# The last norm of a mixture-of-experts block beside the last four experts instead of the last two

## The chip, the cores and the metric

The kernel runs on one core of one Trainium2 chip. The metric is the device time of one execution in microseconds (us), here the median of several runs. The core has five engines with queues of their own: TensorE (PE, matrix products), VectorE (DVE), ScalarE (ACT), GpSimd (POOL) and SyncE (SP, which here only issues DMAs). The profile calls the loading of a product's fixed operand PEld.

## The reference

One block with 2048 tokens of 1024 columns: a mixer (Hyena filters and Fourier mixing), then a hierarchical mixture of experts, then a last norm. Only the last two parts matter here:

```python
g_sel = jnp.argmax(g_logits, axis=-1)                       # one group of 4 for each token
e_logits = jnp.take_along_axis(e_logits, g_sel[:, None, None], axis=1)[:, 0]
top_l, top_i = lax.top_k(e_logits, TOP_K)                   # two of this group's 8 experts
weight = p_group[:, None] * jax.nn.softmax(top_l, axis=-1)
...
    a = xb @ w_gate[e]
    u = xb @ w_up[e]
    y = (jax.nn.silu(a) * u) @ w_down[e]
    return (y * rows_w[:, None].astype(y.dtype)).astype(tok.dtype)
...
x = x + hierarchical_moe(rmsnorm(x, norm2_g[i]), ...)
return rmsnorm(x, final_g)
```

Both choices of a token lie in one group. So two experts of different groups never have a token in common. There are 32 experts with 6 MB of weights each (float32).

## The kernel before

The mixer and the routing take the first half of the span. The routing counts each expert's tokens and sorts the experts by their counts (`order`, on the DVE): the first turns are fixed (experts 0 and 1), the following have many and few tokens in a mixed order, and the last `NLAST` = 2 turns go to the experts with the fewest. An expert has 128 slots for tokens; the ranks below 18 have 32 slots more (`over` and the products L1583 and L1637).

The experts run turn after turn. Turn e, part 0 (`gate_up`) is 8 chunks of weights, part 1 (`down`) is 4; a chunk is 128 x 1024 numbers, 512 KB. The list `turns` sets the order: part 0 of an expert comes before part 1 of the one before it, so that the transposes of an expert's result (`turn_s`) fall into the other's products. At the end before, this order is given up: (29,1), (30,0), (30,1), (31,0), (31,1), with `turn_s` right behind `gate_up`.

`take` hands out the next chunk. At each call it runs one step of the list `ends` if there is one, issues loads for up to 28 chunks ahead on SP's queue, and cuts the chunk that is two ahead. A cut (L1391, L1392) splits float32 into two parts for exact products: ACT writes the high part h, then the low part l = w - h is written by the DVE, or by POOL for the chunks of `POOL_CUTS` and `TAIL_CUTS` (every second chunk from 360 on). Each chunk then takes six products of 128 x 128 by 128 x 512. A loaded chunk lies in one of 24 buffers: of every 24 chunks the first 16 in the ring with the tag `wr`, 8 in two other rings. The buffer is free when the chunk is cut.

An expert's result is added to the rows of X2 (in DRAM) with an indirect DMA by POOL (L1650; L1652 for the tokens beyond 128). These scatter-adds wait for each other.

The last norm is made for all tokens in `bulk`, called when the last expert but two has added its rows: for each of 16 tiles a read of X2 into a `wr` buffer (L1437, on SP), a sum of squares (L1427, on ACT), for each four tiles a short chain of small operations (`rsq`, L242 to L256), a product with the scale and the gain on the DVE (L1453) and a write to the output (L1454, on SP). These are steps in `ends`, so they run beside the last experts' products. The last two experts' tokens get their sums and norm again: `ahead` gathers the rows of X2 (L1472), `finish` adds the product (L1482), writes the sums to X2 (L1483) and norms (L1484, L1486), and at the very end the rows are scattered to the output (L1705). The second of them may share tokens with the first, so its `ahead` comes after the first one's sums.

After all experts a loop runs over blocks of tokens beyond all slots; it has as many rounds as there are such blocks.

The order on each engine and the buffers of a ring are fixed when the program is built, by priority in program order among what is ready; the waits between engines are put in then.

Of the kernel before, what the change touches and what calls it, by code (L numbers as in the profile page):

```python
# [45 lines left out]
# experts are taken by their counts: the first ones get 32 slots beyond the 128  # L46
NFIX = 2
# the first experts' 128 slots take tokens of the first tiles only
FIRST = 14
NLAST = 2  # L50
# [4 lines left out]
TAIL_CUTS = tuple(range(360, 384, 2))  # L55
# [6 lines left out]
def _ranks():  # L62
    """The rank by count of the expert at each turn."""
    n, few = NE - NFIX - NLAST, NE - NOV - NLAST
    many, rest = iter(range(NFIX, NOV)), iter(range(NOV, NE))
    mid = [next(rest) if (i + 1) * few // n > i * few // n else next(many) for i in range(n)]
    return list(range(NFIX)) + mid + list(rest)
# [18 lines left out]
def fft_tables(T):  # L86
    """A transform of 4096 points in two stages: n = 64 a + p, p = 16 m + g, k = r + 64 k2.

    The first one sums over a and turns by exp(-2 pi i r n / 4096), r = 0..31 (r = 0 stands for 0 and 32, both
    real before the turn); the second one sums over p.  # L90
    """
# [11 lines left out]
    w = first(64 * a[None, :, None] + 16 * m[None, None, :] + g[:, None, None])     # [g, a, m, comp]  # L103
    wu = np.zeros((16, 2, 2, 32, 2, 2, 2, 64))      # [g, m % 2, part of z, a, m // 2, pass, m % 2, comp]
# [9 lines left out]
    w = first(32 * np.arange(P)[None, :] + np.arange(32)[:, None]).reshape(32, 64, 2, 64)     # [q, a, x, comp]  # L114
# [25 lines left out]
    # the inverse leaves p in the order 4 g + m  # L140
# [5 lines left out]
def tables():  # L146
# [16 lines left out]
    # real and imaginary parts of a 64-point transform, two groups at once  # L163
# [6 lines left out]
    # transform over t, folded twice: t < 512, bins k = 2 k' + parity  # L170
# [14 lines left out]
    # routing: tokens, counted from one, in the order of their tiles; rows of ranks  # L185
# [6 lines left out]
    # order of the experts: their numbers as tie breakers, ranks of the turns, masks  # L192
# [14 lines left out]
def build(tc, I, out, dbg=None, upto=99):  # L207
# [4 lines left out]
    with es:  # L212
# [8 lines left out]
        # Fourier columns of tiles 0..3 and 8..11; those of tiles 15 - k and 7 - k, with the row that follows, are read backwards  # L221
# [16 lines left out]
        def rsq(dst, src, scale, pool, n, tag, ln=False):  # L238
            """dst = (src * scale + EPS) ** -0.5"""
# [9 lines left out]
            # one Newton step for what the tables leave  # L249
# [8 lines left out]
        # ------------------------------------------------------------------ mixer, first part  # L258
# [15 lines left out]
        with ExitStack() as e1, ExitStack() as e2:  # L274
# [52 lines left out]
            def conv(c, wvec, sink):  # L327
                """Projection chunk c through the short filter, a quarter of t for every call; sink(q, piece)."""
# [33 lines left out]
            def to_rows(src, dst):  # L362
                """[channel, 512 t] to [t, channel] rows of DRAM, in one or two parts, after the next products."""
# [16 lines left out]
            def sinks(c):  # L380
                """Filter and use of chunk c: v (8..11) is kept for x1 (4..7), whose product with it is z."""
# [13 lines left out]
            with tc.tile_pool(name="pa", bufs=1) as pa:  # L395
                # per-channel vectors: short filter (3 x 12), its bias (12), gains of heads and of the first norm
# [57 lines left out]
            def wprime(g):  # L454
                """Fourier columns of the projection, with the transform along a head folded in."""
# [28 lines left out]
            def ktaps(q):  # L484
                """The filter's taps 32 i + q, and the absolute sum so far."""
# [30 lines left out]
            def ksum(kt):  # L516
                """The kernel's absolute sum; the skip weight goes in as a tap at lag 0."""
# [32 lines left out]
            # implicit filters' features: partitions = (half of t, feature)  # L550
# [46 lines left out]
            def spread():  # L597
                """Features of t on the lower half of the partitions, of 2048 - t on the upper one."""
# [44 lines left out]
            def fweights(h):  # L643
                """Weights of half h of the Fourier columns, in two parts."""
# [8 lines left out]
            def fourier(h, i, wh, wl, pm, dst=None):  # L653
                """Fourier columns of tile i, rows = t, to DRAM or to where they are used."""
# [68 lines left out]
            def prod(o, w, xh, xl):  # L723
                """o = w x, both in two parts."""
# [3 lines left out]
            def residue(n):  # L728
# [6 lines left out]
                if n == 0:  # L735
                    # the real bins 0 and 32 and those between them
# [8 lines left out]
                else:  # L745
                    # real parts on the lower half of the partitions, imaginary ones on the upper half
# [35 lines left out]
            def begin(t):  # L782
                """Rows t and 1024 + t of the fold, the first half of the columns where the second one comes straight."""
# [9 lines left out]
            def pair(t):  # L793
                """Sums and differences of rows t and L - t, and of 1024 + t and 1024 - t."""
                rr = rrs.pop(t)
                pq = []
                for k in range(2):
                    # groups of 66 real parts and 62 imaginary ones
# [9 lines left out]
            # Fourier columns, rows = t  # L808
# [41 lines left out]
        # ------------------------------------------------------------------ Fourier mixing, output projection  # L850
        seq = []
        z = NE - NLAST
        turns = [(0, 0)] + [t for e in range(1, z) for t in ((e, 0), (e - 1, 1))]
        turns += [(z - 1, 1), (z, 0), (z, 1), (z + 1, 0), (z + 1, 1)]
# [33 lines left out]
        def gather(e, part=(0, 1)):  # L888
# [4 lines left out]
            if 1 in part and RANK[e] < NOV:  # L893
# [3 lines left out]
                if e < NFIX:  # L897
                    # the queue goes on with these cuts while the rows are unknown
# [3 lines left out]
        # the first gathers come before the last tiles' rows  # L902
# [5 lines left out]
        with ExitStack() as e3:  # L908
# [21 lines left out]
            def headnorm(pool, y, n=P, ln=False):  # L930
                """y [n, 8, 64] in place: every head over its root mean square."""
# [10 lines left out]
            def split_T(pool, y, rev=False):  # L942
                """[t, 512] to hi and lo of its transpose, [128 c, 4, 128 t]."""
# [11 lines left out]
            def mix(yh, yl, wh, wl, h):  # L955
                """Half h of the output columns."""
# [33 lines left out]
            with tc.tile_pool(name="fo", bufs=1, side="right", reuse_waits="tile") as fo:  # L990
# [9 lines left out]
                # t = 512, which is its own partner  # L1000
# [14 lines left out]
                def fold(t, par):  # L1015
                    """Parity par of the bins wants the sum and the difference, the other one the difference and the sum."""
# [94 lines left out]
            with tc.tile_pool(name="pd", bufs=1, side="right", reuse_waits="tile") as pd_:  # L1111
# [11 lines left out]
                # a token's number in two parts and its weight in three, which bfloat16 holds exactly  # L1123
# [27 lines left out]
                def first_rows(dst, src, u):  # L1151
                    """Rows to gather: a slot's token, or the quarter of it that a partition holds."""
# [5 lines left out]
                def order():  # L1158
                    """Experts by their counts: one-hot of the turn of each, and what depends on it."""
# [7 lines left out]
                    V.scalar_tensor_tensor(so[:, 0], cnt, float(NE), srt[:, 0:NE], op0=ALU.mult, op1=ALU.add)  # L1167
                    V.tensor_tensor(so[:, 1], so[:, 0], srt[:, 2 * NE:3 * NE], op=ALU.mult)
# [14 lines left out]
                def route(o0, n):  # L1183
                    """Experts, ranks and slots of n tiles from o0 on."""
# [3 lines left out]
                    def first(src, w, rev, tag):  # L1188
                        """One-hot of the first largest of w."""
# [24 lines left out]
                    # weights of the two choices  # L1214
# [33 lines left out]
                    # an expert's slots get their tokens and weights: one-hot of the rank against that of the expert  # L1248
# [20 lines left out]
                    if o0 + n == FIRST:  # L1269
                        # later tokens of the first experts get no rank below 128  # L1270
# [24 lines left out]
                        # rows to add to; an empty slot adds nothing to a row of its own  # L1295
# [6 lines left out]
                    for k in range(2):  # L1302
                        # the choice's number among all ranks
# [78 lines left out]
        # ------------------------------------------------------------------ experts  # L1382
        if True:
# [3 lines left out]
            def cut(n):  # L1387
# [4 lines left out]
                x = (G if n in POOL_CUTS + TAIL_CUTS else V).tensor_tensor(l, raws[n], h, op=ALU.subtract)  # L1392
# [6 lines left out]
            def take():  # L1399
                """The next chunk of weights; those after it are loaded and cut ahead."""  # L1400
# [28 lines left out]
            def bulk():  # L1429
                """The last norm of all tokens, in steps; those of the experts still at work get theirs again."""  # L1430
# [8 lines left out]
                def sq(o):  # L1439
# [4 lines left out]
                    # the weights' cuts go first  # L1444
# [5 lines left out]
                def scale(o):  # L1450
                    g, n = of[o]
                    x = xts.pop(o)
                    V.scalar_tensor_tensor(x, x, fss[g][1][:, o - g:o - g + 1], fgb, op0=ALU.mult, op1=ALU.mult)  # L1453
                    S.dma_start(out[0, P * o:P * o + P, :], x)  # L1454

                def step(k):
                    for o in range(2 * k, min(2 * k + 2, NT)):
                        read(o)
                    if 0 <= k - 6 < NT:
                        sq(k - 6)  # L1460
                    for o in range(2):
                        if scales:
                            scale(scales.pop(0))
                return [lambda k=k: step(k) for k in range(30)]
# [3 lines left out]

            def ahead(e):
# [352 lines left out]
```

## Time and profile before

| | us |
|---|---|
| median of 3 runs | 1753.75 (1752.33 to 1755.37) |
| profiled execution, first to last instruction (span) | 1749.5 |
| median of the runs above the span | 4.25 |
| PE busy | 1622.4 (93%) |
| DVE busy | 1228.6 (70%) |
| ACT busy | 1040.4 (59%) |
| POOL busy | 477.4 (27%) |

The page gives no time for the profiled execution but its span; what lies around it is taken as 4.25 us, the difference to the median. A group in the profile names its line, engine and operation, then what is written and read, how many there are, their busy time, the mean of one in ns, and the idle time of the engine just before them with what ended it. A row of the timeline begins with its start from the beginning of the span, then its length. Where an engine is held by another, the wait is inside the length that the row shows, not in front of it.

### The profile page before, as it was taken

To read this page: it belongs to the slowest core of one execution; us is meant where nothing else is said; L and a number is where in the kernel's file an instruction comes from. 1 tells how busy PE (TensorE), PEld (TensorE's weight loads), DVE (VectorE), ACT (ScalarE), POOL (GpSimd) and SP (SyncE) were. 2 spreads that over 40 slices of the span, in tenths; PEclk is the share of its full clock that TensorE was granted. 3 is DMA by queue.
4 is the path that set the end of the run, shared out by engine and by line. 5 is a ranking of instruction groups with operands and counts; after the bars stand their busy time and mean duration, and the time that the engine had idled before them with its cause. 6 is when DMAs were issued, how large, how long until landed. Compare 5 with 4: busy or idle time off the path is not lost.

```text
span 1749.5 us, 27286 instructions
## 1 busy us (share of the span) xinstructions
PE 1622.4 (93%) x9043; PEld 1225.8 (70%) x9043; DVE 1228.6 (70%) x2105; ACT 1040.4 (59%) x1694; POOL 477.4 (27%) x512
## 2 busy tenths in 40 slices
PE   7999999999998969999998899999999999999863
PEld 5766666778777848867766667777777777677642
DVE  7576554422899665556888878887888888788666
ACT  8444555545898552215444567776777777667772
POOL 0203444232332232005434222222222222222252
PEclk9999999999999969999998899999999999999986
DMA  7245676899665585478777599999999999999974
GB/s 253 85 124 175 196 220 199 217 281 254 197 202 171 188 278 201 167 199 266 219 257 252 210 372 336 338 339 330 347 336 337 304 355 337 307 334 340 311 285 179
DMA packets 234620, 450.30 MB, mean 257 GB/s; under 512 B 27020, under 2 KB 82277, under 8 KB 233325
## 3 DMA queue, kind: packets, MB, share of 16 engines
q1 hardware_dynamic: 164244, 324.64, 53.6%
q0 software_dynamic: 36384, 97.94, 20.6%
q10 hardware_dynamic: 33848, 25.95, 4.7%
q8 instruction: 73, 1.20, 0.3%
q14 instruction: 71, 0.57, 0.1%
HBM read 346.32 MB, written 103.43 MB: 257 GB/s over the span
## 4 chain that ended last, share of the span: by engine, by line
PE 58%; DMA 9%; DVE 8%; issue 7%; ACT 3%; POOL 2%; SPq 1%; ACTq 0%; POOLq 0%; DVEq 0%
PE pa L1563 17%; PE psd L961 8%; PE py L1631 8%; PE psm L323 6%; PE po L1583 3%; DMA X<-yt,sia 3%; PE po L1637 2%; PE pm L659 2%; PE psEO L1348 2%; PE pstr L1533 1%; PE psEO L983 1%; PE psk L488 1%; DMA YZ<-yz 1%; PE psm L659 1%; POOL acc L496 1%
## 5 line engine op out<-in xcount | busy, mean ns | idle before, releaser
L1392 DVE TENSOR_TENSOR l<-w,h 128x1024 fp32r<-128x1024 f32 x370 | 452.8, 1228 | 144.5 <-ACT h L1391 121.5
L1391 ACT CAST h<-w 128x1024 fp32r<-128x1024 f32 x384 | 402.8, 1050 | 182.0 <-PE pa L1563 130.2
L323 PE MATMUL psm<-hhi,wt 128*128 128x512 f32 x768 | 251.9, 399 | 0.2 <-ACT hhi L425 0.2
L1563 PE MATMUL pa<-l,xh 128*128 128x512 f32 x512 | 207.3, 405 | 22.0 <-DVE l L1392 13.4
L1563 PE MATMUL pa<-h,xh 128*128 128x512 f32 x512 | 209.6, 410 | 1.9 <-ACT xh L1534 1.7
L1563 PE MATMUL pa<-h,xl 128*128 128x512 f32 x512 | 207.1, 405 | 0.0
L323 PEld LDWEIGHTS psm<-hhi,wt 128*128 128x128 f32 x768 | 145.3, 190 | 41.9 <-issue 9.9
L323 PE MATMUL psm<-hlo,wt 128*128 128x512 f32 x384 | 152.7, 398 | 0.1
L1563 PEld LDWEIGHTS pa<-l,xh 128*128 128x128 f32 x512 | 99.2, 194 | 45.4 <-DVE l L1392 15.0
L1563 PEld LDWEIGHTS pa<-h,xh 128*128 128x128 f32 x512 | 99.1, 194 | 40.3 <-ACT xh L1534 6.7
L1563 PEld LDWEIGHTS pa<-h,xl 128*128 128x128 f32 x512 | 99.2, 194 | 25.1 <-issue 3.3
L892 POOL DMA_INDIRECT xg<-XR,gia x30 | 49.7, 1657 | 224.2 <-PE pstr L1533 180.6
L1631 PE MATMUL py<-h,sh 128*128 128x512 f32 x256 | 108.6, 424 | 2.3 <-ACT sh L1608 2.3
L1631 PE MATMUL py<-l,sh 128*128 128x512 f32 x256 | 104.8, 409 | 0.0
L1631 PE MATMUL py<-h,sl 128*128 128x512 f32 x256 | 102.4, 401 | 0.0
L323 PEld LDWEIGHTS psm<-hlo,wt 128*128 128x128 f32 x384 | 73.0, 190 | 20.4 <-issue 5.3
L1650 POOL DMA_INDIRECT X<-yt,sia x30 | 48.2, 1606 | 136.6 <-ACT yt L1646 133.6
L1652 POOL DMA_INDIRECT X<-yo,sib x18 | 38.0, 2111 | 145.7 <-issue 79.0
L720 POOL TENSOR_TENSOR yl<-yl,yh 128x512 fp32r<-128x512 f32 x32 | 46.7, 1464 | 108.0 <-ACT yh L719 83.4
L347 ACT COPY u<-psm 128x512 f32<-128x512 f32 x48 | 28.1, 585 | 78.6 <-PE psm L323 78.6
L1583 PE MATMUL po<-w,xot 128*32 128x256 f32 x1152 | 69.0, 382 | 0.0
L496 POOL TENSOR_TENSOR acc<-ab,acc 128x512 f32<-128x512 f32 x32 | 48.3, 1509 | 68.4 <-ACT ab L495 67.2
(464 smaller groups left out, 3669.3 us busy)
## 6 DMA issues: line engine op xcount, KB each, us to landing
w<-in_w_gate SPq DMA_DIRECT2D x128, 512.0 KB
w<-in_w_up SPq DMA_DIRECT2D x128, 512.0 KB
w<-in_w_down SPq DMA_DIRECT2D x120, 512.0 KB
xt<-in_x SPq DMA_DIRECT2D x31, 512.0 KB
de<-in_c_decay SPq DMA_DIRECT2D x32, 256.0 KB
YK<-yk ACTq DMA_DIRECT2D x32, 256.0 KB
z<-zT POOLq DMA_DIRECT2D x32, 256.0 KB, 5.7
YZ<-yz SPq DMA_DIRECT2D x64, 128.0 KB
```

The lines of the kernel that those rows point to most:

```text
L323: T.matmul(pm, wt[:, a, d, :], b[q][:, d, :], start=n == 0, stop=n == 23)
L496: G.tensor_tensor(KS["acc"], ab, KS["acc"], op=ALU.add)
L659: T.matmul(pm, a[q][:, d, P * o:P * o + P], b[:, d, :], start=n == 0, stop=n == 23)
L720: e.tensor_tensor(yl, y, yh, op=ALU.subtract)
L892: G.indirect_dma_start(xg_[e], None, XR, bass.IndirectOffsetOnAxis(ap=ga[:, e:e + 1], axis=0))
L961: T.matmul(pd, a[:, c, :], b[:, c, 512 * h:512 * h + 512], start=n == 0, stop=n == 11)
L1391: cuts.append(A.copy(h, raws[n]))
L1392: x = (G if n in POOL_CUTS + TAIL_CUTS else V).tensor_tensor(l, raws[n], h, op=ALU.subtract)
L1563: T.matmul(pa[m], x[:, d, :], y[:, f], start=d == 0 and q == 0, stop=d == 7 and q == 2)
L1583: T.matmul(po_[e][32 * j:32 * j + 32, 256 * m:256 * m + 256], xoT[e][:, k, b, :], w[:, 256 * j:256 * j + 256], start=b == 0, stop=b == 3, ...
L1631: T.matmul(py[i], x[:, c, :], y[:, f], start=c == 0 and q == 0, stop=c == 3 and q == 2)
L1650: G.indirect_dma_start(X2, bass.IndirectOffsetOnAxis(ap=sia[:, e:e + 1], axis=0), yt, None, compute_op=ALU.add)
```

## The change

`NLAST` goes from 2 to 4, and the last four turns go to the expert with the fewest tokens of each group (a large number is taken from its sorting key in `order`). The order of the turns is kept mixed to the end. All four `ahead` come at once behind (27,1), into `wr` buffers, and no longer wait for each other; sums and results are issued later. The bulk starts there too, one tile for each step where two were read before. The product of scale and gain is parted: the scale on the DVE, the gain on POOL. No weights are cut on POOL at the end any more. Removed comments are left out here.

```diff
-NLAST = 2
+NLAST = 4
...
-TAIL_CUTS = tuple(range(360, 384, 2))
...
-        turns = [(0, 0)] + [t for e in range(1, z) for t in ((e, 0), (e - 1, 1))]
-        turns += [(z - 1, 1), (z, 0), (z, 1), (z + 1, 0), (z + 1, 1)]
+        turns = [(0, 0)] + [t for e in range(1, NE) for t in ((e, 0), (e - 1, 1))] + [(NE - 1, 1)]
...
                     V.scalar_tensor_tensor(so[:, 0], cnt, float(NE), srt[:, 0:NE], op0=ALU.mult, op1=ALU.add)
+                    low = pd_.tile([P, 4, 1], F32, name="low")
+                    key = so[:, 0].rearrange("p (g e) -> p g e", g=4)
+                    V.tensor_reduce(low, key, axis=AX.X, op=ALU.min)
+                    V.tensor_tensor(so[:, 1].rearrange("p (g e) -> p g e", g=4), key,
+                                    low.to_broadcast([P, 4, 8]), op=ALU.is_equal)
+                    V.scalar_tensor_tensor(so[:, 0], so[:, 1], -float(1 << 18), so[:, 0], op0=ALU.mult, op1=ALU.add)
...
-                x = (G if n in POOL_CUTS + TAIL_CUTS else V).tensor_tensor(l, raws[n], h, op=ALU.subtract)
+                x = (G if n in POOL_CUTS else V).tensor_tensor(l, raws[n], h, op=ALU.subtract)
...
-                    V.scalar_tensor_tensor(x, x, fss[g][1][:, o - g:o - g + 1], fgb, op0=ALU.mult, op1=ALU.mult)
+                    V.tensor_scalar(x, x, fss[g][1][:, o - g:o - g + 1], None, op0=ALU.mult)
+                    G.tensor_tensor(x, x, fgb, op=ALU.mult)
                     S.dma_start(out[0, P * o:P * o + P, :], x)
 
                 def step(k):
-                    for o in range(2 * k, min(2 * k + 2, NT)):
-                        read(o)
+                    if 0 <= k < NT:
+                        read(k)
                     if 0 <= k - 6 < NT:
                         sq(k - 6)
-                    for o in range(2):
-                        if scales:
-                            scale(scales.pop(0))
-                return [lambda k=k: step(k) for k in range(30)]
+                    if scales:
+                        scale(scales.pop(0))
+                return [lambda k=k: step(k) for k in range(-4, 28)]
...
             def ahead(e):
-                za = mw.tile([P, D], F32, tag="xg", bufs=2, name="za")
-                G.indirect_dma_start(za, None, X2, at(sia[:, e:e + 1]))
-                return za
+                zas[e] = mw.tile([P, D], F32, tag="wr", bufs=NRAW, name="za")
+                G.indirect_dma_start(zas[e], None, X2, at(sia[:, e:e + 1]))
...
-                G.indirect_dma_start(X2, at(sia[:, e:e + 1]), za, None)
...
+            def sums(e):
+                G.indirect_dma_start(X2, at(sia[:, e:e + 1]), zas.pop(e), None)
+
+            def result(e):
+                G.indirect_dma_start(out[0], at(sia[:, e:e + 1]), oas.pop(e), None, bounds_check=L - 1, oob_is_err=False)
...
-                    if e >= z:
-                        turn_s(e)
-                elif e < z - 1:
+                elif e < z:
                     down(e, lambda e=e: between(e + 1))
-                elif e == z - 1:
-                    down(e, lambda e=e: turn(e + 2))
-                    ends.extend(bulk())
-                    za = ahead(z)
                 else:
-                    y = down(e, lambda: None)
-                    oas.append(finish(e, y, za))
-                    if e == z:
-                        za = ahead(e + 1)
+                    finish(e, down(e, lambda e=e: between(e + 1)))
...
-            while ends:
-                ends.pop(0)()
-            for e, oa in zip((z, z + 1), oas):
-                G.indirect_dma_start(out[0], at(sia[:, e:e + 1]), oa, None, bounds_check=L - 1, oob_is_err=False)
+                if (e, d) == (z - 1, 1):
+                    ends.extend(bulk())
+                    for x in range(z, NE):
+                        ahead(x)
+                if (e, d) == (z + 1, 1):
+                    sums(z)
+                    sums(z + 1)
+                if (e, d) == (z + 2, 1):
+                    while ends:
+                        ends.pop(0)()
+                    for x in range(z, z + 3):
+                        result(x)
+                    sums(z + 2)
+            result(NE - 1)
+            sums(NE - 1)
```

More of the change, by code (lines that the diff above doesn't have):

```diff
@@ L1167, in order @@
                     V.scalar_tensor_tensor(so[:, 0], cnt, float(NE), srt[:, 0:NE], op0=ALU.mult, op1=ALU.add)
+                    low = pd_.tile([P, 4, 1], F32, name="low")
+                    key = so[:, 0].rearrange("p (g e) -> p g e", g=4)
+                    V.tensor_reduce(low, key, axis=AX.X, op=ALU.min)
+                    V.tensor_tensor(so[:, 1].rearrange("p (g e) -> p g e", g=4), key, low.to_broadcast([P, 4, 8]), op=ALU.is_equal)
+                    V.scalar_tensor_tensor(so[:, 0], so[:, 1], -float(1 << 18), so[:, 0], op0=ALU.mult, op1=ALU.add)
                     V.tensor_tensor(so[:, 1], so[:, 0], srt[:, 2 * NE:3 * NE], op=ALU.mult)
@@ L1452, in scale, with finish @@
                     x = xts.pop(o)
-                    V.scalar_tensor_tensor(x, x, fss[g][1][:, o - g:o - g + 1], fgb, op0=ALU.mult, op1=ALU.mult)
+                    V.tensor_scalar(x, x, fss[g][1][:, o - g:o - g + 1], None, op0=ALU.mult)
+                    G.tensor_tensor(x, x, fgb, op=ALU.mult)
                     S.dma_start(out[0, P * o:P * o + P, :], x)
                 def step(k):
-                    for o in range(2 * k, min(2 * k + 2, NT)):
-                        read(o)
+                    if 0 <= k < NT:
+                        read(k)
                     if 0 <= k - 6 < NT:
                         sq(k - 6)
-                    for o in range(2):
-                        if scales:
-                            scale(scales.pop(0))
-                return [lambda k=k: step(k) for k in range(30)]
+                    if scales:
+                        scale(scales.pop(0))
+                return [lambda k=k: step(k) for k in range(-4, 28)]
             def at(rows):
                 return bass.IndirectOffsetOnAxis(ap=rows, axis=0)
+            zas, oas = {}, {}
             def ahead(e):
-                za = mw.tile([P, D], F32, tag="xg", bufs=2, name="za")
-                G.indirect_dma_start(za, None, X2, at(sia[:, e:e + 1]))
-                return za
-            def finish(e, py, za):
-                ss = mp.tile([P, 1], F32, name="zs")
-                ra = mp.tile([P, 1], F32, name="zra")
-                oa = mp.tile([P, D], F32, tag="yt", bufs=2, name="oa")
+                zas[e] = mw.tile([P, D], F32, tag="wr", bufs=NRAW, name="za")
+                G.indirect_dma_start(zas[e], None, X2, at(sia[:, e:e + 1]))
+            def finish(e, py):
+                za = zas[e]
+                ss = mp.tile([P, 1], F32, tag="zs", bufs=2, name="zs")
+                ra = mp.tile([P, 1], F32, tag="zra", bufs=2, name="zra")
+                oa = oas[e] = mp.tile([P, D], F32, tag="yt", bufs=2, name="oa")
                 for i in range(2):
@@ L1486, in finish @@
                 V.scalar_tensor_tensor(oa, za, ra, fgb, op0=ALU.mult, op1=ALU.mult)
-                return oa
+            def sums(e):
+                G.indirect_dma_start(X2, at(sia[:, e:e + 1]), zas.pop(e), None)
+            def result(e):
+                G.indirect_dma_start(out[0], at(sia[:, e:e + 1]), oas.pop(e), None, bounds_check=L - 1, oob_is_err=False)
             def table():
@@ L1677, in build @@
             turn_s(0)
-            oas = []
             for e, d in turns:
```

## The prediction

> **What bounds the kernel now.** I read the page, then the stretches of the tail, then groups and single instructions in it.
>
> ```profile
> span 1749.5 us, 27286 instructions
> PE   7999999999998969999998899999999999999863
> DVE  7576554422899665556888878887888888788666
> PEclk9999999999999969999998899999999999999986
> ```
>
> TensorE (PE) is busy nine tenths until the last two or three of forty slices, and only there does its clock fall. The stretches of that end, with columns PE, PEld, DVE, ACT, POOL busy, granted clock, DMA share, GB/s:
>
> ```profile
> 1624.70:1652.20 27.50, 27.48 (x148) 20.69 (x143) 22.25 (x22) 21.54 (x27) 7.41 (x4) 1.00 0.94 324
> 1652.20:1667.90 15.70, 9.72 (x30) 7.42 (x29) 3.79 (x5) 6.48 (x8) 8.38 (x4) 0.67 0.69 180
> 1667.90:1682.50 14.60, 10.11 (x38) 7.42 (x37) 6.17 (x11) 11.39 (x19) 8.64 (x4) 0.88 0.93 354
> 1682.50:1731.40 48.90, 28.10 (x87) 20.88 (x86) 46.48 (x51) 28.30 (x44) 19.21 (x8) 0.76 0.69 264
> 1731.40:1749.50 18.10, 0.62 (x3) 0.19 (x1) 3.60 (x8) 1.35 (x3) 2.96 (x3) 0.62 0.24 92
> ```
>
> Until 1652.2 PE is the bound. Then come the last two experts (chunks 360 to 383). VectorE (DVE) is idle for 12 us while cuts on GpSimd (POOL) are late, and from 1682.5 it is busy 46.48 of 48.9 us. So the last norm's stage is bound by DVE, not PE. The first loss, and what bounds the rest:
>
> ```profile
> 1656.85 2.06 POOL L1652 DMA_INDIRECT X<-yo,sib  x1 [5.99 <-DMA X<-yt,sia]
> 1658.37 2.91 POOL L1392 TENSOR_TENSOR l<-w,h 128x1024 fp32r<-128x1024 f32 x1
> 1661.34 0.79 PE L1563 MATMUL pa<-l,xh 128*128 128x512 f32 x1 [5.97 <-POOL l L1392]
> 1722.05 1.12 PE L1607 MATMUL pstr<-ident,s 128*128 128x128 f32 x4 [8.58 <-DVE s L1569]
> 804.63 2.39 POOL L1332 TENSOR_TENSOR xn<-xn,g2b 128x1024 f32<-128x1024 f32 x1 [2.79 <-ACT hr L245]
> 804.67 2.37 DVE L253 TENSOR_TENSOR hv<-hv,hr 128x8 f32<-128x8 f32 x1
> 1710.39 2.39 POOL L1392 TENSOR_TENSOR l<-w,h 128x1024 fp32r<-128x1024 f32 x1
> 1709.69 3.12 DVE L254 TENSOR_TENSOR q4v<-q4v,q4r 128x4 f32<-128x4 f32 x1
> ```
>
> A cut on POOL stood behind a scatter that waited 5.99 us, and PE lost 5.97. At 1722 PE had stood 8.58 us for a product that DVE was late with. The last four rows, two pairs, are the key of this case: a DVE operation on 4 or 8 columns lasts as long as the POOL product beside it, and ends with it (804.63 + 2.39 and 804.67 + 2.37 are both 807.0; 1710.39 + 2.39 and 1709.69 + 3.12 both 1712.8). So a DVE operation with two SBUF inputs and a POOL product take turns.
>
> **The change part by part.** The prices, from groups of the tail or of the whole span (after the bar: busy us, then the mean ns of one):
>
> ```profile
> L1453 DVE SCALAR_TENSOR_TENSOR xt<-xt,frs,fgb 128x1024 f32<-128x1024 f32 x16 | 30.2, 1931 | 0.4
> L1392 DVE TENSOR_TENSOR l<-w,h 128x1024 fp32r<-128x1024 f32 x370 | 452.8, 1228 | 144.5 <-ACT h L1391 121.5 <-DMA w<-in_w_gate 6.7 <-DMA w<-in_w_down 0.4
> L1482 DVE SCALAR_TENSOR_TENSOR za<-py,wsl,za 128x512 f32<-128x512 f32 x4 | 2.8, 745 | 1.6 <-PE py L1631 1.6
> L1486 DVE SCALAR_TENSOR_TENSOR oa<-za,zra,fgb 128x1024 f32<-128x1024 f32 x2 | 2.6, 1278 | 0.0
> L1609 DVE TENSOR_TENSOR sl<-pstr,sh 128x512 fp32r<-128x512 f32 x2 | 1.4, 692 | 2.0 <-ACT sh L1608 1.9
> L1569 DVE TENSOR_TENSOR s<-s,pa 128x512 f32<-128x512 f32 x2 | 1.3, 674 | 0.0
> L1535 DVE TENSOR_TENSOR xl<-pstr,xh 128x512 fp32r<-128x512 f32 x2 | 1.3, 677 | 0.0
> L253 DVE TENSOR_TENSOR q4v<-q4v,q4r 128x4 f32<-128x4 f32 x4 | 0.6, 162 | 0.1
> L1332 POOL TENSOR_TENSOR xn<-xn,g2b 128x1024 f32<-128x1024 f32 x14 | 33.5, 2392 | 66.0 <-ACT xn L1331 58.2 <-DMA xo<-x0T 4.0 <-ACT hr L245 2.8
> L416 DVE TENSOR_SCALAR xt<-xt,rs 128x1024 f32<-128x1024 f32 x16 | 11.8, 748 | 0.1
> ```
>
> *Cuts.* Twelve cuts leave POOL (2.39 us each, the DVE held meanwhile) for the DVE (1.23): 12 x 1.16 = 13.9 us less for the pair. *Scaling.* A tile costs 1.28 now (L1486 is the same operation undisturbed; L1453's 1931 holds waits). It becomes a product with a scalar, 0.75 by L416, and POOL's product with the gain, 2.39 by L1332: 3.14, or 16 x 1.86 = 29.8 us more. Does the scalar product also take turns with POOL? No row has the two together, so 0.75 (held) or 0 (free) of each counts, 12 us apart for sixteen; I take held, as every row of large DVE work on SBUF beside POOL shows it.
>
> On the same point the Trainium skill, "SBUF — State Buffer", section "SBUF: two separate sides", says that a GpSimd operation and a DVE one in a two-port mode, or with two SBUF inputs, exclude each other for a whole instruction; the two pairs of rows agree, for the second kind. By that rule the scalar product is held too, the sum below stands, and moving DVE work to POOL buys nothing here.
>
> *Two more finishes* (`finish` for four experts, not two): each 2 x 0.745 + 1.28 and about six small operations at 0.16, 3.7 us, less the two L1646 copies on ACT that fall away. Two more `ahead`, `sums` and `result` on POOL, two scatter-adds fewer. The bulk's sixteen reads and sixteen writes are as many as before; begun at once they would meet weights at a DMA share of 0.94, later one of 0.69 to 0.93, so I cost the transfers at nothing and only their waits; without that cover a read is late by what lies ahead of it in SP's queue, a chunk or two.
>
> *Order.* (31,0) now runs before (30,1), so the transposes of an expert's product lie in the middle of another's second product, and the wait of 8.58 us goes as such, but PE still waits where DVE is late with cuts. Three small operations join `order()`, on the way to the third expert: 3 x 0.16 = 0.5 by L253, or 2.4 more if one is held as L253 was at 804.67; the first two experts' products lie beside it, so between 0 and 2.9; I take 0.5. By the reference's routing of its input, no expert from turn 18 on has over 128 tokens in either order, so no spare block runs.
>
> *When the bulk can start.* It is called after (27,1), sixteen chunks earlier. But its tiles need slots of the weights' ring:
>
> ```profile
> 1645.89 10.23 DMA X<-yt,sia
> SPq L1437 <- DVE l L1392: 9.4, 3, 6.3
> SPq L1437 <- POOL l L1392: 8.8, 4, 4.5
> 1667.90 27.73 SPq L1437 DMA_DIRECT2D xt<-X  x16
> 1682.51 9.12 DVE L1453 SCALAR_TENSOR_TENSOR xt<-xt,frs,fgb 128x1024 f32<-128x1024 f32 x4
> 1399.37 5.74 PE pa L1563 x24
> ```
>
> Reads already wait for cuts to free a slot (the two SP rows): 16 of them take 27.73 us. Of 24 weight buffers 16 are of this ring. At chunk 344 they hold 346 to 351 and 360 to 369; six come free, and chunks 370, 371 and the four `za` tiles take them. The next to come free are 360's and later; 372 to 375, earlier in the program, take the first four. So the first read gets 364's slot, 19 chunks on. A chunk is 5.74 / 4 = 1.43 us of PE, 27.2 in all; the DVE needs 19 x 1.23 + one finish 3.7 + four halves at 0.68 = 29.8, so 30. If slots were free at once, the read would go when the scatter-add has landed, some 12 us after the start; both ends are kept.
>
> **The sum**, in the profiled execution's time (span 1749.5):
> 1. Before has 40 chunks left at 1624.7. After has as many, with one expert of over 128 tokens less half done: 1626.
> 2. First read 1656 (bound 1638).
> 3. From the first read to the first scaled tile 1682.5 - 1667.9 = 14.6, now 1670.6. PE is then at chunk 372, and nine cuts are left.
> 4. From there the pair DVE and POOL is the bound: 9 x 1.23 = 11.1, 16 x 3.14 = 50.2, two L1486 2.6: 63.9. DVE work on PSUM or on small tiles (four L1482 3.0, small operations 36 x 0.16 = 5.8, L1569 and L1609 1.4) is 10.2, of which I hide half under POOL's products: 69.0. The last of it ends at 1739.6, 5.1 either way, 12 earlier if scalar products are free.
> 5. Then the results:
>
> ```profile
> 1734.38 1.00 POOL L1705 DMA_INDIRECT out_y<-oa,sia  x1 [0.30 <-issue]
> 1738.62 0.98 POOL L1705 DMA_INDIRECT out_y<-oa,sia  x1 [3.24 <-DMA out_y<-oa,sia]
> DMA to landing us min/median/max: 3.2/3.3/3.5
> ```
>
> Each scatter to the output waits for the one before, 4.24 us apart, and the first for all tiles' rows. Now there are four behind the bulk instead of two: landing 3.4, three steps 12.7, from the last issue to the end 10.9, `sums` behind it 1.0: 28.0 if a bulk tile is last; 22 if the last tile lies some 6 us (one finish and two cuts) ahead of the last finish. I take 25: 1764.6. (`oa` has two buffers, so expert 30's norm waits for 28's scatter; its 3.9 us fit into the steps.)
> 6. The three runs' median is 4.25 above the span (1753.75 - 1749.5); with the 0.5: 1769.4, say **1770**, 0.9% slower.
>
> The gain that the change makes is real in this sum: the waits of 1652 to 1682 (PE idle 15.7 - 9.72 + 14.6 - 10.11 = 10.5 us) go. The pair's work from 1626 on, 38 cuts 46.7 + 50.2 + four L1486 5.1 = 102, against before's 26 x 1.23 + 12 x 2.39 + 16 x 1.28 + 2.6 = 83.8, eats it, and two more steps at the end come on top.
>
> **The rivals.**
> *Packed* (0.17): slots come early, the bulk fills the DVE from chunk 350 on, and the last finish, not a tile, is last. Then 1626 + 102 + half of 20.2 of other DVE work, and 12.2 to the end (0.3 to the last scatter, the 10.9 and 1.0 of step 5): 1750.3, 1754.5 with what lies around; 1744.5 if all the other work hides. It needs the first read before some 1645. The SP rows speak against it.
> *Side by side* (0.08, the other side: faster). POOL's gain products run beside the DVE. Place: L1453's successor; price: 16 x 2.39 = 38.2 from 1670.6, 1708.8, and the 28.0: 1736.8, 1741. It decides once POOL's products delay DVE operations by under about 1 us each. The two pairs of rows speak against it; PSUM-sourced DVE work speaks for a little.
> *Queue order* (0.12): `sums` of 28 and 29 wait on POOL for the last read, which waits for slots that come free only with rows written; gain products stand behind them, as the cut stood behind L1652. One or two such waits of 6 to 10 us: 1786.
> *Nothing done* (0.03): the end is set elsewhere; 1754.
>
> **How the numbers follow.** The forecast has 0.60, own range 1760 to 1780. 0.2% (3.5 us) is what a measurement can tell from no change. Faster: side by side 0.08 and half of packed, 0.17. Same: the rest of packed and nothing done, 0.11. Slower: the other two, 0.72. The range 1747 to 1786 leaves out some 0.13 below and 0.06 above.
>
> **What would show it.** Right: DVE over nine tenths busy from about 1670 to the end; L1453's successors on the DVE with means well above 0.75 or cuts above 1.23; POOL products of 2.4 us or more, sixteen; the first X2 read 15 us or more after the last scatter-add's landing; four output scatters about 4.2 us apart after the last tile. Wrong: reads that start at 1640, PE above nine tenths until 1700, or DVE operations of 0.75 and 1.23 in the middle of POOL products.

## The result and the profile after

| | before | after |
|---|---|---|
| median | 1753.04 us | 1772.53 us |
| lowest to highest of 4 runs | 1752.23 to 1755.37 | 1764.98 to 1774.55 |
| span of the profiled execution | 1749.5 | 1772.8 |

The changed kernel takes 1.0106 times as long (95% interval 1.0085 to 1.0128): 1.1% slower. The forecast was 1770.

The page of the changed kernel, with its span in forty slices:

```profile
span 1772.8 us, 27358 instructions
PE   7999999999989879999997999999999999999830
DVE  7576555322899675547888778887787778788992
```

PE now keeps nine tenths until three slices from the end. The DVE, not PE, is full in the two slices ahead of the last. The same stretches, cut at the events of this trace (first read of X2, first scaled tile, last product with the gain, end); the columns are PE, PEld, DVE, ACT, POOL busy, granted clock, DMA share, GB/s:

```profile
1626.00:1658.30 32.30, 31.02 (x142) 24.59 (x141) 29.19 (x35) 27.93 (x34) 7.71 (x6) 1.00 0.88 309
1658.30:1680.60 22.30, 19.66 (x85) 14.13 (x84) 20.21 (x31) 21.07 (x31) 0.00 (x0) 1.00 0.99 384
1680.60:1743.80 63.20, 17.86 (x52) 12.39 (x51) 51.96 (x48) 21.47 (x35) 45.27 (x18) 0.63 0.58 215
1743.80:1772.80 29.00, 0.00 (x0) 0.00 (x0) 4.38 (x12) 2.70 (x6) 5.87 (x6) 0.50 0.29 114
```

Up to 1680.6 PE is busy 50.7 of 54.6 us: of the 10.5 us that it stood idle between 1652 and 1682, 3.9 are left. What was won there is lost in the third row. For 63 us the DVE and POOL are both busy most of the time (51.96 and 45.27), PE gets 17.86 us of work, and its granted clock falls to 0.63. Then 29 us follow without PE. Groups of the DVE in this third stretch (busy us, mean ns of one, idle time before):

```profile
L1458 DVE TENSOR_SCALAR xt<-xt,frs 128x1024 f32<-128x1024 f32 x16 | 25.8, 1672 | 0.2
L1397 DVE TENSOR_TENSOR l<-w,h 128x1024 fp32r<-128x1024 f32 x8 | 17.5, 2220 | 0.0
L1489 DVE SCALAR_TENSOR_TENSOR za<-py,wsl,za 128x512 f32<-128x512 f32 x4 | 3.0, 743 | 3.0 <-PE py L1643 3.0
L242 DVE TENSOR_SCALAR q4v<-fss 128x4 f32<-128x4 f32 x3 | 2.6, 872 | 0.0
L253 DVE TENSOR_TENSOR q4v<-q4v,q4r 128x4 f32<-128x4 f32 x3 | 2.1, 706 | 0.1
```

Single instructions of it, with start and length, DVE and POOL:

```profile
1680.64 6.94 DVE L1458 TENSOR_SCALAR xt<-xt,frs 128x1024 f32<-128x1024 f32 x4
1687.51 3.36 DVE L1397 TENSOR_TENSOR l<-w,h 128x1024 fp32r<-128x1024 f32 x1
1690.79 0.68 DVE L1581 TENSOR_TENSOR s<-s,pa 128x512 f32<-128x512 f32 x1
...
1695.24 0.16 DVE L242 TENSOR_SCALAR q4v<-fss 128x4 f32<-128x4 f32 x1
...
1726.31 2.30 DVE L242 TENSOR_SCALAR q4v<-fss 128x4 f32<-128x4 f32 x1
```

```profile
1681.83 11.27 POOL L1459 TENSOR_TENSOR xt<-xt,fgb 128x1024 f32<-128x1024 f32 x4 [36.12 <-ACT jk L1432]
...
1720.37 10.51 POOL L1459 TENSOR_TENSOR xt<-xt,fgb 128x1024 f32<-128x1024 f32 x4 [7.01 <-DVE xt L1458]
...
1735.54 1.25 POOL L1495 DMA_INDIRECT X<-za,sia  x1 [0.16 <-issue]
1736.82 6.93 POOL L1459 TENSOR_TENSOR xt<-xt,fgb 128x1024 f32<-128x1024 f32 x3
```

Each group of four products with the gain on POOL starts about a microsecond after the DVE's first scaled tile, and from then on the DVE's work is stretched: four scalar products take 6.94 us where 4 x 0.75 = 3.0 is their cost alone, and a cut of 1.23 takes 3.36. An operation on four columns takes 2.30, and the same one 0.16 at 1695.24, between two groups of POOL's products.

### The profile page after: what moved, and what is told of

It is laid out like the page before. It is cut to its first block, busy times and chain, and to the rows that moved or that the text cites. A ratio compares the mean times of both kernels' runs of the same rounds, so it can differ in the third digit from the quotient of the medians.

```text
span 1772.8 us, 27358 instructions
## 1 busy us (share of the span) xinstructions
PE 1614.7 (91%) x9043; PEld 1219.6 (69%) x9043; DVE 1248.4 (70%) x2136; ACT 1043.0 (59%) x1698; POOL 492.1 (28%) x520
## 5 line engine op out<-in xcount | busy, mean ns | idle before, releaser
L1397 DVE TENSOR_TENSOR l<-w,h 128x1024 fp32r<-128x1024 f32 x382 | 475.0, 1250 | 118.3 <-ACT h L1396 91.4
L1575 PE MATMUL pa<-l,xh 128*128 128x512 f32 x512 | 203.2, 397 | 5.8 <-DVE l L1397 5.8
L1575 PE MATMUL pa<-h,xl 128*128 128x512 f32 x512 | 203.3, 397 | 0.0
L891 POOL DMA_INDIRECT xg<-XR,gia x30 | 50.0, 1668 | 225.1 <-PE pstr L1545 189.1
L1643 PEld LDWEIGHTS py<-l,sh 128*128 128x128 f32 x256 | 49.4, 193 | 31.0 <-DVE l L1397 22.3
```

The lines of the kernel that those rows point to most:

```text
L891: G.indirect_dma_start(xg_[e], None, XR, bass.IndirectOffsetOnAxis(ap=ga[:, e:e + 1], axis=0))
L1397: x = (G if n in POOL_CUTS else V).tensor_tensor(l, raws[n], h, op=ALU.subtract)
L1575: T.matmul(pa[m], x[:, d, :], y[:, f], start=d == 0 and q == 0, stop=d == 7 and q == 2)
L1643: T.matmul(py[i], x[:, c, :], y[:, f], start=c == 0 and q == 0, stop=c == 3 and q == 2)
```

## The experiments

The theory ("turns"): POOL's product and DVE work on SBUF run one after the other, so the sixteen products with the gain, and before them the twelve cuts, cost the pair their whole length. Its rivals are named at each run. The ratios are to the kernel before on the same chip. Differences in us are between medians; taken from the ratios they differ by up to some 3 us.

### One product on the DVE again, in the changed kernel (e1) and its reverse in the kernel before (e2)

```diff
-                    V.tensor_scalar(x, x, fss[g][1][:, o - g:o - g + 1], None, op0=ALU.mult)
-                    G.tensor_tensor(x, x, fgb, op=ALU.mult)
+                    V.scalar_tensor_tensor(x, x, fss[g][1][:, o - g:o - g + 1], fgb, op0=ALU.mult, op1=ALU.mult)
```

> The changed kernel, but a tile's scale and gain are one DVE operation again, as before the change. Turn theory (a POOL product and a DVE operation exclude each other, so the parted product costs 3.14 us a tile of their common time against 1.28): 16 x 1.86 = 29.8 us less of common work. The stretch from the first scaled tile (1680.6) to the last (1743.8) shrinks from 63.2 to some 35 us, and the median from 1772.5 to 1742 to 1752. Length theory (late reads and four scatters one after another set the end, whatever engine multiplies): 8 us less at most, 1764 or more.

The second kernel makes the opposite edit in the kernel before, so that only the parting of the product is added to it.

> The kernel before the change, with one thing of the change: the scale on the DVE, the gain on POOL. Turn theory: 29.8 us of common work more in a stretch that is bound by it (DVE busy 46.48 of 48.9 us), so 1753 becomes 1775 to 1785. Rival: POOL has room there (19.2 of 48.9 us busy), and the DVE is relieved by 16 x 0.53 = 8.5 us: 1745 to 1753.

Measured: e1 1746.24 us, ratio 0.9972 (0.9953 to 0.9991); e2 1774.69 us, ratio 1.0137 (1.0105 to 1.0169). So the parted product alone costs 22.4 us in the kernel before (its median there 1752.28), and taking it out of the changed kernel wins about 26 (1772.53 - 1746.24; 23.5 by the two ratios). The rest of the change, without it, makes the kernel 0.3% faster. In e1 the stretches from the first scaled tile on, and the two large DVE groups of the first of them, are:

```profile
1679.00:1713.50 34.50, 16.27 (x52) 11.94 (x50) 33.73 (x48) 21.30 (x35) 2.49 (x3) 0.78 0.97 382
1713.50:1743.80 30.30, 0.00 (x0) 0.00 (x0) 4.37 (x12) 2.70 (x6) 5.66 (x6) 0.50 0.31 125
```

```profile
L1458 DVE SCALAR_TENSOR_TENSOR xt<-xt,frs,fgb 128x1024 f32<-128x1024 f32 x16 | 19.5, 1281 | 0.1
L1397 DVE TENSOR_TENSOR l<-w,h 128x1024 fp32r<-128x1024 f32 x8 | 9.6, 1213 | 0.0
```

The stretch is 34.5 us in place of 63.2, with the same sixteen tiles and eight cuts. Of the 28.7 us between them, 6.3 lie in the scalar products (25.8 - 19.5), 7.9 in the cuts (17.5 - 9.6), some 4 in the small operations, and 10.5 in idle time of the DVE (63.20 - 51.96 against 34.50 - 33.73), for the most part the end of the stretch, where only POOL's products are left. The tail behind the stretch is as long as in the changed kernel, 30.3 and 29.0. The turns theory holds.

### No weights cut on POOL, in the kernel before (e3, and the same again as e3b)

```diff
-TAIL_CUTS = tuple(range(360, 384, 2))
+TAIL_CUTS = ()
```

> The kernel before the change, with one thing of the change: all cuts of the last two experts on the DVE, none on POOL. Turn theory: a cut on POOL holds the DVE for 2.39 us, one on the DVE takes 1.23, so 12 x 1.16 = 13.9 us less, and the wait of 5.97 us of PE at 1661 for a cut that stood behind a scatter goes too: 1733 to 1742. Rival: the POOL cuts did relieve the DVE, which gets 12 x 1.23 = 14.8 us more: 1760 to 1768.

> e3_cuts_dve once more (before, all cuts on the DVE), to stand beside the next two: 1739 to 1744 if its first median of 1741.6 holds.

Measured: 1741.55, ratio 0.9952 (0.9933 to 0.9971), and on another chip 1742.95, ratio 0.995 (0.9933 to 0.9967). This one line makes the kernel before 0.5% faster, against 0.3% for e1, though the intervals overlap. Its stretches, with the first two cut as those of before, its cut after the long gap, its first scaled tiles, and ACT's wait:

```profile
1652.20:1667.90 15.70, 5.41 (x24) 4.07 (x22) 3.25 (x3) 4.29 (x6) 3.64 (x3) 0.74 0.59 149
1667.90:1682.50 14.60, 9.12 (x29) 6.86 (x29) 11.34 (x16) 13.69 (x22) 0.00 (x0) 0.69 1.00 396
1682.50:1718.30 35.80, 23.55 (x75) 17.65 (x75) 35.12 (x54) 22.83 (x37) 3.56 (x2) 0.76 0.81 299
...
```

```profile
1668.11 1.23 DVE L1392 TENSOR_TENSOR l<-w,h 128x1024 fp32r<-128x1024 f32 x1 [12.27 <-ACT h L1391]
...
1677.13 4.87 DVE L1453 SCALAR_TENSOR_TENSOR xt<-xt,frs,fgb 128x1024 f32<-128x1024 f32 x4
```

```profile
ACT jk L1427 <- DMA xt<-X: 12.3, 2, 11.4
```

The span shrinks by 13.2 us (1749.5 to 1736.3). The third stretch is 13.1 shorter, but it does not hold the same work: four of the sixteen tiles are scaled before it begins. From the first scaled tile to the end of the last it is 39.8 us (1677.13 to 1716.89), and was 47.2 (1682.51 to 1729.75): 7.5 of the 13.2 us lie there, and 5.4 in the earlier start. PE's gap from 1652 to 1668 is not gone: PE is busy 5.41 us there, less than before (9.72). Now ACT stands 11.4 us in a square for the first read of X2, and the cuts wait behind it. So POOL's cut behind a scatter-add was the wait that showed, and another wait stood behind it that keeps the DVE's next cut still longer (12.27 us of idle time, 10.0 before). What e3 wins, it wins without closing that gap.

### The bulk four chunks later, on top of e3 (e7, e9)

```diff
-                return [lambda k=k: step(k) for k in range(30)]
+                return [lambda: None] * 4 + [lambda k=k: step(k) for k in range(30)]
```

> e3_cuts_dve (1741.6; two last experts, all cuts on the DVE), with the bulk's steps begun four chunks later. In e3 ACT's first sum of squares waited 11.4 us for a read of X2 with the cuts of weights behind it in ACT's queue, and PE stood from 1657 to 1670. Queue theory: begun later, the cuts go first, and PE runs on: 5 to 10 us less, 1731 to 1737. Rival: the DVE's work after 1670 is the bound (busy 19.96 of 20 us), so the gap is only moved, and the bulk ends later by what it begins later: 0 to 4 us more.

Measured 1745.89, ratio 0.9955 (0.9939 to 0.9972): nothing won over e3. The waits of e7:

```profile
ACT jk L1427 <- DMA xt<-X: 8.3, 1, 8.3
PE py L1631 <- ACT sh L1608: 9.6, 2, 8.8
```

The gap moved rather than closed: ACT still waits 8.3 us for the first read, and now PE waits 8.8 for the copy `sh` behind it. e9 put the first squares behind that copy with one more edit on top of e7:

```diff
-                A.copy(sh, pt)
+                cuts.append(A.copy(sh, pt))
```

> e7_later_bulk (1745.9), with the sums of squares put behind expert 30's cut sh in ACT's queue. In e7 ACT waited 8.3 us for a read of X2 ahead of sh, and PE stood 9 us for sh. Queue theory: that wait goes, and PE's work of expert 30's second product begins 9 us earlier: 4 to 8 us less, 1738 to 1742. Rival: the bulk's last group, not PE, sets the end, as it was last in e7: 0 to 2 us less.

Measured 1749.78, ratio 0.9985 (0.9974 to 0.9997). In its trace the square still stands ahead of the copy, after an idle of 8.61 us:

```profile
1673.79 1.06 ACT L1427 ACTIVATE jk<-xt 128x1024 f32<-128x1024 f32 x1 [8.61 <-DMA xt<-X]
1674.84 0.57 ACT L1608 CAST sh<-pstr 128x512 fp32r<-128x512 f32 x1
```

So the edit did not bring about the order it was for. e9 is inconclusive: what ACT's order would be worth stays open, and so does why it lies 6.8 us above e3b on the same chip.

### Reads of X2 earlier, in the changed kernel (e4)

Of the four gathered tiles `za` only one is left in the ring of the weights; the others go to other buffers. That frees slots for the first reads.

```diff
-                zas[e] = mw.tile([P, D], F32, tag="wr", bufs=NRAW, name="za")
+                if e == z:
+                    zas[e] = mp.tile([P, D], F32, tag="zo", name="za")
+                elif e == z + 1:
+                    zas[e] = mw.tile([P, D], F32, tag="wr", bufs=NRAW, name="za")
+                else:
+                    zas[e] = mw.tile([P, D], F32, tag="xg", bufs=2, name="za")
```

> The changed kernel, but only one of the four gathered sums lies in the ring of the weights (one has a buffer of its own, two take the ring of the experts' tokens). Slot theory: the four took the slots that the next loads and the reads wait for (SP's load L879 waited 20.7 us in the changed kernel). Three slots more let the first read of X2 go three chunks, some 4.3 us, earlier than 1658.3. If only that start set the end, the median falls by the same 4 us, to 1767 to 1769. Turn theory: DVE and POOL have the same common work, and the DVE was already 8.3 to 9.9 of 10 us busy from 1650 on, so 0 to 3 us less: 1769 to 1773.

Measured 1770.14, ratio 1.0087 (1.0067 to 1.0108). The first read, on SP, and the first and last operations of the bulk in e4:

```profile
1655.54 1.53 SPq L1442 DMA_DIRECT2D xt<-X  x2
```

```profile
1674.47 6.93 DVE L1458 TENSOR_SCALAR xt<-xt,frs 128x1024 f32<-128x1024 f32 x4
...
1736.70 6.93 POOL L1459 TENSOR_TENSOR xt<-xt,fgb 128x1024 f32<-128x1024 f32 x3
```

The first tile is scaled 6.2 us earlier than after the change (1680.64), and the last three products with the gain begin 0.12 earlier (1736.82) and end at 1743.6. Thirteen cuts, not eight, now lie behind the first scaled tile: what starts earlier puts off as much other work of the DVE. The work of the pair sets the end, not its start. The span is 1773.0, as without the edit; 2.4 us between the medians is within what the runs scatter.

### Fewer results at the end (e5, e8)

e5 is the changed kernel without the output scatters of experts 28, 29 and 30, so it leaves out the last norm of these experts' tokens in their final form.

```diff
-                    for x in range(z, z + 3):
-                        result(x)
```

> The changed kernel without the output scatters of experts 28, 29 and 30 (left out: the rows of their tokens keep what the bulk wrote; expert 31's scatter stays). Serial theory: the three scatters cost their three steps of 4 us at the end, and expert 30's and 31's norms no longer wait for a buffer: 11 to 15 us less, 1757 to 1762. Rival: the sums' scatters and the loop behind them set the end, and the output scatters run beside them: 0 to 4 us less.

Measured 1759.4, ratio 1.0043 (1.0026 to 1.0059): 13.1 us less than after the change (11.0 by the ratios). In its trace the time behind the last product with the gain is 17.2 us (1739.21 to 1756.4) in place of 29.05: 11.85 less, 3.95 for each scatter left out; the rest lies ahead of that product. e8 is e1 with the last three experts in place of four in the new arrangement; it computes everything.

```diff
-NLAST = 4
+NLAST = 3
...
                 if (e, d) == (z + 1, 1):
                     sums(z)
-                    sums(z + 1)
-                if (e, d) == (z + 2, 1):
                     while ends:
                         ends.pop(0)()
-                    for x in range(z, z + 3):
+                    for x in range(z, z + 2):
                         result(x)
-                    sums(z + 2)
+                    sums(z + 1)
```

> e1_gain_dve (the change with scale and gain in one DVE operation, 1746.2) with three last experts instead of four. Serial theory: one output scatter and one scatter of sums fewer at the end is one step of 4 us: 1740 to 1744. Rival: the bulk starts twelve chunks later in the work, its cover of PE work is shorter, and what the step saves is given back: 1745 to 1750.

Measured 1742.09, ratio 0.9952 (0.9934 to 0.9969): 4.2 below e1, but the intervals of the two overlap. The traces are clearer: behind the end of the last tile's scaling e1 has 30.35 us (from 1713.45) and e8 25.5 (from 1709.83), 4.9 less, for one output scatter and one scatter of sums fewer. Output scatters, first the four of the changed kernel, then the three of e8:

```profile
1749.37 0.99 POOL L1499 DMA_INDIRECT out_y<-oa,sia  x1 [0.30 <-issue]
1753.15 0.98 POOL L1499 DMA_INDIRECT out_y<-oa,sia  x1 [2.79 <-DMA out_y<-oa,sia]
1757.21 0.97 POOL L1499 DMA_INDIRECT out_y<-oa,sia  x1 [3.08 <-DVE oa L1492]
...
1761.21 0.98 POOL L1499 DMA_INDIRECT out_y<-oa,sia  x1 [3.02 <-DMA out_y<-oa,sia]
```

```profile
1716.54 0.99 POOL L1498 DMA_INDIRECT out_y<-oa,sia  x1 [9.47 <-DMA out_y<-xt]
1720.08 0.99 POOL L1498 DMA_INDIRECT out_y<-oa,sia  x1 [2.55 <-DMA out_y<-oa,sia]
1724.11 0.97 POOL L1498 DMA_INDIRECT out_y<-oa,sia  x1 [3.05 <-DVEq L1723]
```

They follow each other 3.5 to 4.1 us apart in both: about one of issue, then the landing of the one before.

### Results ahead of sums, in e1 (e6)

```diff
-                oa = oas[e] = mp.tile([P, D], F32, tag="yt", bufs=2, name="oa")
+                oa = oas[e] = (mp.tile([P, D], F32, tag="yt", bufs=2, name="oa") if e < NE - 2 else
+                               mw.tile([P, D], F32, tag="xg", bufs=2, name="oa"))
...
-                if (e, d) == (z + 1, 1):
-                    sums(z)
-                    sums(z + 1)
...
                         result(x)
-                    sums(z + 2)
+                        sums(x)
```

> e1_gain_dve (1746.2) with the last part changed: experts 30 and 31 norm into buffers of their own, and each output scatter stands in POOL's queue ahead of the same expert's scatter of sums, where e1 had three scatters of sums ahead (1706 to 1719) and the first output scatter at 1720.4. Serial theory: the first output scatter goes when the last tile's rows have landed, at about 1717, and the next follow 4.2 us apart without a wait for a norm: 2 to 5 us less, 1741 to 1744. Rival: the steps of the output scatters alone set the end and their start is fixed by the landing of the sums: 0 to 1 us less.

Measured 1746.64, ratio 0.9961 (0.9931 to 0.9991): no gain over e1 (1746.24). The order that the edit meant did not come about in POOL's queue:

```profile
1719.42 0.95 POOL L1495 DMA_INDIRECT X<-za,sia  x1 [5.41 <-DMA X<-za,sia]
1720.79 0.99 POOL L1499 DMA_INDIRECT out_y<-oa,sia  x1 [0.41 <-issue]
```

All four scatters of sums still stand ahead of the first output scatter, which goes at 1720.79 (e1: 1720.36). So the run shows no gain from more buffers for `oa` alone, and says nothing on the order.

## Why the prediction was right

The sign and the mechanism came out as forecast, and the time nearly (1770, measured 1772.53), but this last in part by luck: the span was off by 8 us, and what stands around it made up for most of that (step 6). By its steps:

*Turns.* e1 and e2 show that the parted product is the loss: 26 us out of the changed kernel, 22.4 into the kernel before. The prediction had 29.8 for it. The one point for which it had no row, whether a product with a scalar is held too, came out as it took it: L1458's mean is 1.672 us, where the same operation alone was 0.748. But its price was too high. POOL's products, least, median and greatest in ns:

```profile
L1459 POOL TENSOR_TENSOR xt<-xt,fgb x16: 2332/2773/3352, 1681.8 to 1741.4; 128x1024 f32<-128x1024 f32 x16
```

The shortest are the last three, with the DVE idle; the median is one beside a scalar product that is held. So a held scalar product added some 0.44 us to POOL's, not 0.75, and a tile cost the pair about 2.8, not 3.14. An estimate from this, 16 x (2.8 - 1.28) = 24 us, is close to what e1 and e2 measured; with it e2 would have been expected at 1776, and not at 1775 to 1785. Why it adds less than its own length is open.

By the Trainium skill, "SBUF — State Buffer", section "SBUF: two separate sides", this was to be expected for an operation in a two-port mode; and "VectorE: DVE Perf Modes", section "Mode 2×_2P — use both read ports for one tensor", has a float32 product with a scalar in such a mode. The trace agrees: 0.748 us alone against 1.228 for a cut with two inputs of the same size, and held beside POOL.

*Cuts.* 13.9 us were put down for twelve cuts less on POOL. e3's median is 10.7 less, its profiled span 13.2. The three small operations in `order()` took 0.54 together, for 0.5.

*Steps 1 and 2, the start and the first read.* 1656 was forecast, 1658.34 measured, by the wait for slots that it named. SP's queue in the changed kernel, its wait and the two issues around it:

```profile
SPq L879 <- DVE qav L251: 20.7, 1, 20.7
```

```profile
1651.89 5.68 SPq L879 DMA_DIRECT2D w<-in_w_up  x4
...
1658.34 0.35 SPq L1442 DMA_DIRECT2D xt<-X  x1
```

A weight load stands 20.7 us for a slot, up to 1651.89, and the reads wait behind it. *Packed* needed reads before 1645, and fell with that. e4 adds that an earlier start would not have helped.

*Step 3, from the first read to the first scaled tile: mis-sized.* 14.6 us, taken from before, measured 22.3 (1658.34 to 1680.64). Before, ACT was busy 11.39 of the 14.6 us; here it is busy 21.07 of the 22.3, and the squares of the tiles lie between its cuts. ACT in the changed kernel, three of the first four squares:

```profile
1663.77 1.06 ACT L1432 ACTIVATE jk<-xt 128x1024 f32<-128x1024 f32 x1 [1.20 <-DMA xt<-X]
...
1667.18 1.06 ACT L1432 ACTIVATE jk<-xt 128x1024 f32<-128x1024 f32 x1
...
1674.20 1.04 ACT L1432 ACTIVATE jk<-xt 128x1024 f32<-128x1024 f32 x1
```

They come some 3.5 us apart. From the end of the fourth, at 1675.24, to the first scaled tile another 5.4 us go to `rsq`'s small operations, with cuts between them. That the cuts set this length is read from these rows; no run tested it.

*Step 4, the pair's stretch: mis-sized the other way.* 69.0 was forecast, 63.1 measured (1680.64 to 1743.75, the end of the last product with the gain). As the start was 10 us later, one cut of the nine had been made before it (1.2), and two norms of results that were counted here (2.6) came only behind it: the DVE stands from 1736.6 to 1754.09, as the row below shows, since ACT waits 24 us for a buffer of `oa` that 28's output scatter frees. The other 2.1 us are the net of several things and were not taken apart further: the lower price of a held scalar product makes the stretch shorter, while 3.0 us in which the DVE waits for PE (L1489) and the scatter between POOL's products make it longer. Little DVE work hid beside POOL's products by being on PSUM: of that work only L1581 ran inside one, and L1489 ran between the groups.

```profile
1754.09 0.15 DVE L242 TENSOR_SCALAR qav<-zs 128x1 f32<-128x1 f32 x1 [17.49 <-ACT oa L1490]
```

```profile
1752.91 1.06 ACT L1490 ACTIVATE oa<-za 128x1024 f32<-128x1024 f32 x1 [24.06 <-DMA out_y<-oa,sia]
```

The misses of steps 3 and 4 have opposite signs; with the late read they add up to 4.2 us: 1743.75 against 1739.6. One of the signs named failed here: the DVE was to be over nine tenths busy to the end, and was busy 51.96 of 63.2 us, as it waits 3 us for PE and has nothing to do beside POOL's last three products.

*Step 5, the results: mis-sized.* 25 was taken between 22 and 28; measured 29.05 (1743.75 to 1772.8). A bulk tile was last, the case of 28.0. The three steps between the scatters are 11.84 (12.7 forecast) and the last issue to the end 11.59 (10.9). The first output scatter comes 5.62 us after the last product, not 3.4: two scatters of sums stand ahead of it in POOL's queue.

```profile
1743.91 0.98 POOL L1495 DMA_INDIRECT X<-za,sia  x1 [0.17 <-issue]
1748.10 0.97 POOL L1495 DMA_INDIRECT X<-za,sia  x1 [3.21 <-DMA X<-za,sia]
```

The first goes right behind the last product, the second waits for it to land. So *Queue order* was right that `sums` would wait in POOL's queue, and the last three products with the gain did stand behind one of them, the scatter at 1735.54, for 1.4 us; the output scatters stood behind two, for some 2 us. Neither is the 6 to 10 us of that rival. The price of each more scatter, 4.24 by the forecast, is 3.95 by e5's trace and 4.9 by e8's, which also has one scatter of sums fewer.

*Step 6, around the span: mis-sized.* 4.25 was the difference between the median and the span of another execution. The profiled run of the changed kernel took 1774.55, 1.75 above its own span, and in the experiments the profiled runs lie 1.77 to 1.95 above theirs. This is where luck comes in: the span was forecast as 1765.1 with `order()`'s 0.5 and came out as 1772.8, 7.7 longer, but the term around it was 2.5 too large, the profiled run lay 2.0 above the median, and 1769.4 had been rounded up.

*The gain of closing PE's gap* (10.5 us of idle time, 3.9 now) did come in the trace, but the reading behind it was only half right. The prediction put PE's loss down to the cut on POOL behind a scatter-add. e3 has no such cut, and PE loses more there, behind ACT's square that waits for the read. What closes the gap in the changed kernel is the four-expert arrangement. Its whole worth, without the parted product and with the cuts off POOL on both sides, is e1 against e3 on one chip: 1746.24 against 1741.55, a loss of about 4.7, for two more scatters at the end, 8 to 10 by e5 and e8, less some 3 to 5 for the gap. This last figure is a difference of differences, and no run measured it by itself.

So the change splits into cuts off POOL (-10.7), the arrangement (about +5) and the parted product (about +26); by the ratios, -8.4, +3.5 and +23.5. e3 and e8 (1742 to 1743 and 1742.1) are the best kernels found, and nothing tells them apart.

## What to carry to other kernels

Before work is given to POOL to relieve a full DVE, look in the trace for a short DVE operation beside a POOL product on SBUF: if it lasts as long as the product and ends with it, the two take turns, and the move costs POOL's length less what it saves the DVE, here 1.4 to 1.6 us a tile. A stage that ends in scatters which wait for each other pays each of them in full, so one more result at the end must win back its landing. When one named wait is taken away, ask which operand of the next engine was as late; here a square stood ready to take the place of the cut.

## What had not been expected of the hardware

The prediction's two pairs were small operations with two inputs. L242, a scalar operation on 128 x 4 with one, was held as well: it took 2.30 us at 1726.31 beside POOL's product, and 0.16 at 1695.24. Nor does the DVE always get the turn between two POOL operations: in e2, L254 on 128 x 4 took 5.32 us at 1718.03, and ended with the second of two cuts on POOL (1718.63 to 1723.32). POOL pays as well: its sixteen products had a mean of 2.716 us, against 2.33 to 2.35 for the last three, with the DVE idle.

An operation with an input in PSUM is not seen to be held. L1581 took 0.68 at 1690.79, inside POOL's group of 1681.83 to 1693.10, as it did before (0.674). In e2 two of 128x512 ran one after the other inside one product on POOL, at 0.7 each:

```profile
1688.15 2.80 POOL L1454 TENSOR_TENSOR xt<-xt,fgb 128x1024 f32<-128x1024 f32 x1
1688.66 1.40 DVE L1483 SCALAR_TENSOR_TENSOR za<-py,wsl,za 128x512 f32<-128x512 f32 x2
```
